# A gated MoBA-attention and mLSTM layer in split float32 on one core: another place for the stationary weights in their buffers, and another schedule for three side jobs

## The chip, the cores and the metric

One core of a Trainium2 chip. A core has TensorE (PE, matmuls, with weight loads shown as PEld), VectorE (DVE), ScalarE (ACT), GpSimd (POOL) and SyncE (SP, which here only issues transfers). Each works through its own instructions in order; they meet at semaphores. The metric is the device time of one execution in microseconds, the median over runs.

## What is computed

The layer has one batch, 256 tokens, width 1024, and all weights are float32. Cut to what matters:

```
ada = c @ w_ada + b_ada;  shift, scale, gate = split(ada)
h   = rmsnorm(x) * (1 + scale) + shift
qa ka va za qm km vm zm om ig fg ga gm = split(h @ w_in)
ya  = (attention(rmsnorm(qa), rmsnorm(ka), va) * silu(za)) @ w_att_proj
qm, km = split(silu(causal_conv4(concat(qm, km))))
hm  = rmsnorm(sigmoid(om) * mlstm(qm, km, vm, ig, fg))
ym  = (hm * silu(zm)) @ w_ml_proj
out = x + gate * ((sigmoid(ga) * ya + sigmoid(gm) * ym) @ w_out)
```

With 256 tokens, attention is causal attention over one block with a relative bias.

## The kernel before, in words

**Split products.** Every large product is made of three float32r matmuls: each operand is split into a high part and the rest (`wh`, `wl` of the weights, `hTh`, `hTl` of h), and high x high, rest x high and high x rest are summed. ScalarE makes `wh` by a cast of the loaded `raw` tile (line 501), VectorE makes `wl = raw - wh` (line 505), or GpSimd for the eight steps in `pool_lo`.

**Steps.** After a first phase (norm, modulation, the projections qa and ka) the work is a list `place` of steps. A step is 256 rows of the contraction by 512 columns of weights; `split(g + 4)` prepares step g + 4 while step g's matmuls are issued. The order of the segments is va (3 parts), za, qm, km, att, zm, vm, then om mixed with the first half of ga, then ga, gm, ml, out. A segment has two halves of 512 columns with four steps each. Steps are numbered from va's first: za starts at 12, qm at 20, km at 28, att at 36, zm at 44, vm at 52.

**Two ways round.** In za, qm, km, att, ga, gm and ml (`kind="ws"`) the weights are stationary: a step has 24 matmuls, each with a weight load of 128 x 128 from `wh` or `wl` and 256 columns of h (or of ya in att, of ym in ml) moving (lines 1160, 1162, 1163). In va, zm, vm and om the weights move, 512 columns at a time (lines 1153 to 1155, 1136 to 1138), and out goes by 256 columns (lines 1146, 1173 to 1175).

**Buffers.** `wh` and `wl` have five buffers each of `RING` = 1152 floats, of which 1024 are used; for `ws` steps the used part begins at float `WS_AT`, so at byte 320 of the buffer. In the built program every such buffer begins at a multiple of 512 bytes, `hTh` and `hTl` 256 bytes past one, and `yah`, `yal`, `ymh`, `yml` at one. So a stationary tile lies 64 bytes (modulo 512) beyond its moving one in the projections of h, and 320 beyond in att and ml. In out, the stationary `yh` and `yl` lie at 64 and 192 and the moving weights at 0. There are six `raw` tiles of 1 MB; SyncE fills them in a fixed order, a load going out when the last reader of the tile it takes over is done.

**Accumulators.** PSUM holds two accumulators `mm` for segment halves. The one of att's first half is that of km's first half, free when km's first half has been convolved. `conv` (line 718) does this in two parts q of 2 x 128 channels: ScalarE starts the sum (line 729), VectorE adds three shifted taps for two channel groups, six instructions (line 735).

**Hooks.** Side jobs hang on steps with `at(step, fn, ...)`; they are issued after `split` and ahead of the step's matmuls. Three of them are touched by the change:

- *Output gate.* `gate_init` (line 947) spreads c over the partitions. `gate_acc(j)` (line 952) is one VectorE reduction over 128 x 1024 (line 954) of the gate's weights with c; there are eight, two for each of four 1 MB loads, and a load's `raw` tile is free after its second reduction. `GSEG` says ahead of which segments the loads stand, and the reductions come four and three steps ahead of those segments.
- *Sums of h.* om is computed by seven block products instead of eight; for that `h_full` (two VectorE sums) and `h_sum` (four) form sums of blocks of h, which `h_high` and `h_low` split in vm.
- *Sums of om's weights.* `om_sum` (line 762) forms sums of weight blocks in DRAM by transfers that GpSimd issues: plain copies (line 769) and adding ones (line 767), eight sums of two halves each, `OM_SUMS`. Later ones read earlier ones; the first reader in SBUF comes with om.

Of the kernel before, what the change touches and what calls it, by code (L numbers as in the profile page):

```python
# [21 lines left out]
NEG = -1e30  # L22
BUCKETS = 32

RING, WS_AT = 1152, 80

COL = dict(qa=0, ka=1024, va=2048, za=3072, qm=4096, km=5120, vm=6144, zm=7168, om=8192,
           ig=9216, fg=9220, ga=9224, gm=10248)
# [23 lines left out]
OM_FIRST = (0, 1, 4, 5)  # L52
OM_SUMS = ((0, (0, 0), False), (2, (0, 1), False), (0, (0, 1), True), (2, (1, 1), True),
           (1, 0, False), (1, (1, 1), True), (3, 1, False), (3, (1, 0), True))
OM_SUM_AT = 6
W_PIECES = ((0, 512), (512, NR), (512, 1024), (1024, NR))


# [13 lines left out]
def tile_hybrid(ctx: ExitStack, tc: tile.TileContext, x, c, params2, w_row, w_va, ada_mod, ada_gate,  # L72
# [62 lines left out]
    adat, wrow, wsp, hf = {}, {}, {}, {}  # L135
# [102 lines left out]
    for j in range(4):  # L238
        n, q = divmod(j, 2)
        nc.tensor.matmul(pc[:, n, q * 256:(q + 1) * 256], pick[:, j:j + 1].to_broadcast([128, 128]), cparts,  # L240
                         start=q == 0, stop=q == 1, skip_group_check=True)
# [129 lines left out]
    def start(name, half=0):  # L371
        return G0[C[name, half]]

    def done(name, half):
        return GE_[C[name, half]]
# [6 lines left out]
    def add_load(fn):  # L382
        loads.append(fn)
        return len(loads) - 1

    def raw_tile():
        return rawp.tile([128, 2048], F32, name="raw")
# [3 lines left out]
    def mk_single(i, q):  # L391
        def f():
            v = raw_tile()[:, 0:4 * NV]
            nc.sync.dma_start(v, w_va[i, q])
            return v.rearrange("p (k n) -> p k n", k=4)
        return f

    def mk_pair(src, c0, kp):
        def f():
            t = raw_tile()  # L400
            v = t.rearrange("p (k n) -> p k n", k=2)
            nc.sync.dma_start(v, src[:, 2 * kp:2 * kp + 2, c0:c0 + 1024])
            return v
        return f

    def mk_quad(src, c0, q):
        def f():
            v = raw_tile().rearrange("p (k n) -> p k n", k=4)
            nc.sync.dma_start(v, src[:, 4 * q:4 * q + 4, c0:c0 + 512])
            return v  # L410
        return f
# [7 lines left out]
    def mk_block(blk):  # L419
        def f():  # L420
            v = raw_tile().rearrange("p (k n) -> p k n", k=4)
            if isinstance(blk, int):
                for hf in range(2):
                    nc.sync.dma_start(v[:, 2 * hf:2 * hf + 2], om_sums[blk][hf])
            else:
                nc.sync.dma_start(v, om_block(*blk))
            return v
        return f

    NSINGLE = 3  # L430
    GSEG = ("km", "att", "zm", "vm")
    gate_loads = []
    for g, (i, kp) in enumerate(place):
        ch = chunks[i]
        if kp == 0 and ch["name"] in GSEG and ch["half"] == 0:
            gate_loads.append(add_load(mk_pair(ada_gate, 0, len(gate_loads))))
        if ch["kind"] == "sums":
            if kp == 0:
                add_load(mk_block(ch["blk"]))
            raw_of[g] = (len(loads) - 1, slice(2 * kp, 2 * kp + 2), slice(0, 512))  # L440
        elif i < NSINGLE or ch["name"] == "ga":
            if kp % 2 == 0:
                quad[i] = add_load(mk_single(i, kp // 2) if i < NSINGLE else mk_quad(ch["src"], ch["c0"] + 512 * ch["half"], kp // 2))
            raw_of[g] = (quad[i], slice(2 * (kp % 2), 2 * (kp % 2) + 2), slice(0, ch["n"]))
        else:
            if ch["half"] == 0:
                pair[ch["name"], kp] = add_load(mk_pair(ch["src"], ch["c0"], kp))
            c0 = 512 * ch["half"]
            raw_of[g] = (pair[ch["name"], kp], slice(0, 2), slice(c0, c0 + 512))
        last_use[raw_of[g][0]] = g  # L450
# [59 lines left out]
    def at(step, fn, *a):  # L510
        hooks.setdefault(step, []).append((fn, a))
# [466 lines left out]
    def ev_out(pt, c0, n, t):  # L978
# [6 lines left out]
        if m < n:  # L985
# [4 lines left out]
              zm=ev_zm, vm=ev_vm, ga=ev_ga, gm=ev_gm)  # L990
# [28 lines left out]
    for nm in ("qm", "km"):  # L1019
        for hf in range(2):  # L1020
            s = done(nm, hf)
# [6 lines left out]
    s = start("zm")  # L1028
    for half in range(2):
        at(s + 5 * half, ml_split, half)  # L1030
        at(s + 5 * half + 3, ml_scores, 2 * half)
        at(s + 5 * half + 4, ml_scores, 2 * half + 1)
    at(start(GSEG[0]) - 10, gate_init)
    gate_left = {}
    for q, nm in enumerate(GSEG):
        s = start(nm) - 4
        at(s, gate_acc, 2 * q)
        at(s + 1, gate_acc, 2 * q + 1)
        gate_left[s + 1] = gate_loads[q]
    at(start("ga"), gate_write)  # L1040
    at(start("gm") + 1, gate_read)
    for q in range(4):
        at(start("ml") + 3 + q, gate_columns, q)
    for q, (i, src, add) in enumerate(OM_SUMS):
        for hf in range(2):
            at(OM_SUM_AT + 5 * q + 2 * hf, om_sum, i, src, add, hf)
    T["A"] = {}
    s = start("att", 1)
    for kh in range(2):
        at(s + 1 + kh, h_full, kh)  # L1050
    for q, name in enumerate(("P5", "P7", "P6", "P3")):
        at(s + 3 + q, h_sum, name)
    s = start("vm") + 1
    for q, name in reversed(list(enumerate(("P5", "P6", "P3", "P7")))):
        at(s + q, h_high, name)
# [1 line left out]
    for hp in range(2):  # L1057
        s = done("om", 6) + 2 * hp
# [29 lines left out]
    for g in range(NG):  # L1088
        ci, kp = place[g]
        ch = chunks[ci]  # L1090
# [39 lines left out]
        for kk in range(2):  # L1130
# [8 lines left out]
            elif ch["name"] == "out":  # L1139

                for i in (0, 1):
                    for t, c0 in ((0, 0), (0, 256), (1, 0), (1, 256)):
                        a = (sh_, sl_)[i][:, k, t * 128:(t + 1) * 128]
                        cs = slice(c0, c0 + 256)
                        for w in (wh, wl)[:2 - i]:
                            nc.tensor.matmul(mmt[ci][:, t, cs], a, w[:, kk, cs],  # L1146
                                             start=first and i == 0 and c0 == 0 and w is wh,
# [82 lines left out]
```

## Time and profile before

| | us |
|---|---|
| median of 3 runs | 351.18 |
| lowest, highest | 350.91, 352.48 |
| the profiled execution | 352.73 |
| its span, first to last instruction | 350.9 |

The profile is of one execution. A row of the timeline has the start in us, the duration in us, the engine, the line, the operation, what it writes and reads, and in brackets how long the engine had been idle and who ended that. A matmul's end is modelled and overlaps the next one's start, so the pace of matmuls is read from start to start.

### The profile page before, as it was taken

What the parts mean: (1) busy time and instruction counts of PE and PEld (TensorE: products, weight loads), DVE (VectorE), ACT (ScalarE), POOL (GpSimd) and SP (SyncE); (2) the same over time, 40 slices, a digit from 0 to 9 for tenths busy, and PEclk for the clock granted to TensorE, in tenths of its full rate; (3) what the DMA queues carried; (4) which work ended last, traced back from release to release, by engine and by line L of the source; (5) the groups of instructions that cost most, each with busy time, mean ns of one, the idle gap of its engine ahead of it and who ended that gap; (6) DMA issues with size and microseconds to landing.
All of it is one profiled execution on the core that took longest, in us unless ns stands there. A gap on an engine that the chain in (4) does not pass through costs nothing.

```text
span 350.9 us, 6244 instructions
## 1 busy us (share of the span) xinstructions
PE 344.8 (98%) x2420; PEld 322.6 (92%) x2420; DVE 265.2 (76%) x393; ACT 220.1 (63%) x344; POOL 99.1 (28%) x97
## 2 busy tenths in 40 slices
PE   7999999999999999999999999999999999999995
PEld 7787889999999999999998888888989999999995
DVE  6989987976993439878988895777777456789842
ACT  4868789799777866574627374668573463565410
POOL 4700003953403473674405172000002131202000
PEclk9999999999999999999999999999999999999999
DMA  8999999894794978799799856677999027444011
GB/s 300 416 414 415 414 418 419 241 391 146 256 325 140 241 200 280 232 389 272 269 337 347 294 193 227 224 277 274 144 283 375 4 75 299 168 169 192 2 62 60
DMA packets 29069, 89.33 MB, mean 255 GB/s; under 512 B 3368, under 2 KB 5296, under 8 KB 28336
## 3 DMA queue, kind: packets, MB, share of 16 engines
q1 hardware_dynamic: 26008, 80.02, 63.1%
q0 software_dynamic: 2880, 8.39, 10.3%
q10 hardware_dynamic: 152, 0.53, 0.5%
q8 instruction: 19, 0.31, 0.3%
q14 instruction: 10, 0.08, 0.1%
HBM read 87.68 MB, written 9.64 MB: 277 GB/s over the span
## 4 chain that ended last, share of the span: by engine, by line
PE 91%; DVE 4%; ACT 2%; issue 1%; POOL 1%; POOLq 0%; ACTq 0%; DVEq 0%
PE mm L1160 13%; PE pm L203 13%; PE mm L1162 13%; PE mm L1163 13%; PE mm L1153 6%; PE mm L1154 6%; PE mm L1155 6%; PE mm L1146 3%; PE aux L1136 2%; PE aux L1137 2%; PE aux L1138 2%; DVE kmT L735 1%; PE xps L268 1%; PE aux L695 1%; PE mm L1174 1%; PE mm L1175 1%
## 5 line engine op out<-in xcount | busy, mean ns | idle before, releaser
L505 DVE TENSOR_TENSOR wl<-raw,wh 128x1024 fp32r<-128x1024 f32 (+1 forms) x98 | 123.7, 1281 | 50.3 <-ACT wh L501 50.1
L501 ACT CAST wh<-raw 128x1024 fp32r<-128x1024 f32 (+1 forms) x106 | 105.5, 1015 | 30.8 <-PE mm L1155 12.0
L1160 PE MATMUL mm<-hTh,wh 128*128 128x256 f32 x320 | 90.2, 282 | 0.0
L1163 PE MATMUL mm<-hTh,wl 128*128 128x256 f32 x320 | 88.9, 278 | 0.0
L1162 PE MATMUL mm<-hTl,wh 128*128 128x256 f32 x320 | 88.9, 278 | 0.0
L1162 PEld LDWEIGHTS mm<-hTl,wh 128*128 128x128 f32 x320 | 60.3, 189 | 0.2
L1160 PEld LDWEIGHTS mm<-hTh,wh 128*128 128x128 f32 x320 | 60.3, 188 | 0.2
L1163 PEld LDWEIGHTS mm<-hTh,wl 128*128 128x128 f32 x320 | 60.1, 188 | 0.0
L1153 PE MATMUL mm<-wh,hTh 128*128 128x512 f32 (+1 forms) x112 | 40.5, 362 | 0.0
L1154 PE MATMUL mm<-wl,hTh 128*128 128x512 f32 (+1 forms) x112 | 40.2, 359 | 0.0
L1155 PE MATMUL mm<-wh,hTl 128*128 128x512 f32 (+1 forms) x112 | 40.2, 359 | 0.0
L505 POOL TENSOR_TENSOR wl<-raw,wh 128x1024 fp32r<-128x1024 f32 x8 | 21.0, 2631 | 15.8 <-ACT wh L501 15.8
L1155 PEld LDWEIGHTS mm<-wh,hTl 128*128 128x128 f32 x112 | 21.0, 188 | 2.5
L1153 PEld LDWEIGHTS mm<-wh,hTh 128*128 128x128 f32 x112 | 21.1, 188 | 2.4
L1154 PEld LDWEIGHTS mm<-wl,hTh 128*128 128x128 f32 x112 | 21.1, 188 | 2.4
L188 ACT CAST wrh<-raw 128x512 fp32r<-128x512 f32 (+1 forms) x24 | 18.2, 761 | 8.0 <-DMA raw<-in_w_row_dram 8.0
L193 DVE TENSOR_TENSOR wrl<-raw,wrh 128x512 fp32r<-128x512 f32 (+1 forms) x26 | 20.5, 813 | 1.3 <-ACT wrh L188 1.3
L203 PE MATMUL pm<-wrh,hTh 128*128 128x512 f32 x64 | 20.0, 393 | 0.0
L203 PE MATMUL pm<-wrh,hTl 128*128 128x512 f32 x64 | 19.9, 392 | 0.0
L841 POOL TENSOR_TENSOR attT<-attT,gat 128x1024 f32<-128x1024 f32 x2 | 5.3, 2635 | 50.3 <-ACT gat L840 50.3
L203 PE MATMUL pm<-wrl,hTh 128*128 128x512 f32 x64 | 19.3, 396 | 0.0
L1160 PE MATMUL mm<-yah,wh 128*128 128x256 f32 x64 | 18.1, 282 | 0.4 <-DVE kmT L735 0.4
(244 smaller groups left out, 753.3 us busy)
## 6 DMA issues: line engine op xcount, KB each, us to landing
raw<-in_w_in_dram SPq DMA_DIRECT2D x31, 1024.0 KB, 8.1
adat<-in_ada_mod_dram SPq DMA_DIRECT2D x16, 512.0 KB, 8.8
om_sum<-in_w_in_dram POOLq DMA_DIRECT2D x12, 512.0 KB, 8.8
raw<-in_w_va_dram SPq DMA_DIRECT2D x6, 688.0 KB, 8.9
raw<-in_ada_gate_dram SPq DMA_DIRECT2D x4, 1024.0 KB, 8.9
raw<-in_w_att_proj_dram SPq DMA_DIRECT2D x4, 1024.0 KB, 8.2
raw<-om_sum SPq DMA_DIRECT2D x8, 512.0 KB, 4.3
raw<-in_w_ml_proj_dram SPq DMA_DIRECT2D x4, 1024.0 KB, 5.8
```

Of the source, the lines that this page charges most:

```text
L188: copy(wsp[k][0][:, c0:c1], wrow[k][:, c0:c1])
L193: e.tensor_tensor(l[:, cs], wrow[k][:, cs], h[:, cs].bitcast(F32), op=OP.subtract)
L203: nc.tensor.matmul(pm[ch][:, t], a[:, k, t * 128:(t + 1) * 128], b[:, cs], start=k == 0 and i == 0, stop=k == KT - 1 and i == 2)
L501: nc.scalar.copy(h, w)
L505: e.tensor_tensor(l, w, h.bitcast(F32), op=OP.subtract)
L1146: nc.tensor.matmul(mmt[ci][:, t, cs], a, w[:, kk, cs], start=first and i == 0 and c0 == 0 and w is wh, stop=last and i == 1 and c0 > 0, sk ...
L1153: nc.tensor.matmul(o, a, wh[:, kk], start=first, stop=False)
L1154: nc.tensor.matmul(o, a, wl[:, kk], start=False, stop=False)
L1155: nc.tensor.matmul(o, b, wh[:, kk], start=False, stop=last)
L1160: nc.tensor.matmul(o, wh[:, kk, cs], sh_[:, k], start=first and i % 2 == 0, stop=False, skip_group_check=True)
L1162: nc.tensor.matmul(o, wh[:, kk, cs], sl_[:, k], start=False, stop=False, skip_group_check=True)
L1163: nc.tensor.matmul(o, wl[:, kk, cs], sh_[:, k], start=False, stop=last and i % 2 == 1, skip_group_check=True)
```

## The change

It does four things.

1. `WS_AT` goes from 80 to 96 floats: stationary weights begin at byte 384 of their buffers. A stationary tile then lies 128 bytes (modulo 512) beyond its moving one in the projections of h, 384 in att and ml. The buffers stay where they are, and so does every other tile.
2. The gate's four loads stand ahead of qm (two), zm and vm instead of km, att, zm and vm, and the reductions are hung on steps 20 and 21, 22 and 23, 40 and 41, 44 and 45; before, on 24 and 25, 32 and 33, 40 and 41, 48 and 49.
3. `h_full` goes from steps 41 and 42 to 25 and 29, `h_sum` from 43 to 46 to 37, 39, 41 and 43.
4. The sums in DRAM get a step each from a list: first halves at 5, 8, 11, 14, 20, 26, 32, 38, second halves three steps later; before, at 6, 11, 16 and so on to 41, second halves two steps later.

```
-RING, WS_AT = 1152, 80
+RING, WS_AT = 1152, 96
...
-OM_SUM_AT = 6
+OM_SUM_AT = (5, 8, 11, 14, 20, 26, 32, 38)
...
-    GSEG = ("km", "att", "zm", "vm")
+    GSEG = ("qm", "qm", "zm", "vm")
...
-        if kp == 0 and ch["name"] in GSEG and ch["half"] == 0:
-            gate_loads.append(add_load(mk_pair(ada_gate, 0, len(gate_loads))))
+        if kp == 0 and ch["half"] == 0:
+            for _ in range(GSEG.count(ch["name"])):
+                gate_loads.append(add_load(mk_pair(ada_gate, 0, len(gate_loads))))
...
-    at(start(GSEG[0]) - 10, gate_init)
+    at(start("qm") - 2, gate_init)
     gate_left = {}
-    for q, nm in enumerate(GSEG):
-        s = start(nm) - 4
+    for q, s in enumerate((start("qm"), start("qm") + 2, start("att", 1), start("zm"))):
         at(s, gate_acc, 2 * q)
         at(s + 1, gate_acc, 2 * q + 1)
         gate_left[s + 1] = gate_loads[q]
...
-    for q, (i, src, add) in enumerate(OM_SUMS):
+    for (i, src, add), step in zip(OM_SUMS, OM_SUM_AT):
         for hf in range(2):
-            at(OM_SUM_AT + 5 * q + 2 * hf, om_sum, i, src, add, hf)
+            at(step + 3 * hf, om_sum, i, src, add, hf)
     T["A"] = {}
-    s = start("att", 1)
     for kh in range(2):
-        at(s + 1 + kh, h_full, kh)
+        at(start("qm", 1) + 1 + 4 * kh, h_full, kh)
     for q, name in enumerate(("P5", "P7", "P6", "P3")):
-        at(s + 3 + q, h_sum, name)
+        at(start("att") + 1 + 2 * q, h_sum, name)
```

In the changed kernel the lines between the load list and the hooks (437 to 1033) have numbers one higher, and those behind the hooks (from 1053 on, the matmuls among them) one lower.

TensorE and ScalarE have the same instructions in the same order before and after. VectorE's order at the convolutions of km's first half, before (`ISA raw,gcol` is a gate reduction, followed by the read of its sum; `wl` belongs to `split`):

```order
194 L735 SCALAR_TENSOR_TENSOR kmT<-mm,prm_68,kmT 128x255 x2
195 L735 SCALAR_TENSOR_TENSOR kmT<-mm,prm_68,kmT 128x254 x2
196 L735 SCALAR_TENSOR_TENSOR kmT<-mm,prm_68,kmT 128x253 x2
197 L954 ISA raw,gcol<-raw,cbg,prm_68 128x1024
198 L954 ISA gcol 128x1
199 L505 TENSOR_TENSOR wl<-raw,wh 128x1024
200 L735 SCALAR_TENSOR_TENSOR kmT<-mm,prm_68,kmT 128x255 x2
201 L735 SCALAR_TENSOR_TENSOR kmT<-mm,prm_68,kmT 128x254 x2
202 L735 SCALAR_TENSOR_TENSOR kmT<-mm,prm_68,kmT 128x253 x2
203 L954 ISA raw,gcol<-raw,cbg,prm_68 128x1024
```

and at the same place after:

```order
200 L736 SCALAR_TENSOR_TENSOR kmT<-mm,prm_68,kmT 128x255 x2
201 L736 SCALAR_TENSOR_TENSOR kmT<-mm,prm_68,kmT 128x254 x2
202 L736 SCALAR_TENSOR_TENSOR kmT<-mm,prm_68,kmT 128x253 x2
203 L506 TENSOR_TENSOR wl<-raw,wh 128x1024
204 L736 SCALAR_TENSOR_TENSOR kmT<-mm,prm_68,kmT 128x255 x2
205 L736 SCALAR_TENSOR_TENSOR kmT<-mm,prm_68,kmT 128x254 x2
206 L736 SCALAR_TENSOR_TENSOR kmT<-mm,prm_68,kmT 128x253 x2
```

The reductions between and behind the two convolutions have left. VectorE at the start of qm's convolutions, before (`yf` is attention's product with the gate za):

```order
169 L701 TENSOR_TENSOR yf<-aux,zat 128x512
170 L505 TENSOR_TENSOR wl<-raw,wh 128x1024
171 L701 TENSOR_TENSOR yf<-aux,zat 128x512
172 L505 TENSOR_TENSOR wl<-raw,wh 128x1024
173 L701 TENSOR_TENSOR yf<-aux,zat 128x512
174 L735 SCALAR_TENSOR_TENSOR qmT<-mm,prm_68,qmT 128x255 x2
```

and after:

```order
172 L506 TENSOR_TENSOR wl<-raw,wh 128x1024
173 L702 TENSOR_TENSOR yf<-aux,zat 128x512
174 L955 ISA raw,gcol<-raw,cbg,prm_68 128x1024
175 L955 ISA gcol 128x1
176 L506 TENSOR_TENSOR wl<-raw,wh 128x1024
177 L702 TENSOR_TENSOR yf<-aux,zat 128x512
178 L955 ISA raw,gcol<-raw,cbg,prm_68 128x1024
179 L955 ISA gcol 128x1
180 L955 ISA raw,gcol<-raw,cbg,prm_68 128x1024
181 L955 ISA gcol 128x1
182 L736 SCALAR_TENSOR_TENSOR qmT<-mm,prm_68,qmT 128x255 x2
```

Four reductions now stand ahead of qm's first convolution: three in these rows, and the first two rows further up, behind the `yf` before. SyncE's loads from za's third on, before (`md` and `NM` belong to the mLSTM's gates):

```order
40 L402 DMA raw<-in_w_in_dram 128x2x1024 x6
41 L402 DMA raw<-in_ada_gate_dram 128x2048
42 L402 DMA raw<-in_w_in_dram 128x2x1024
43 L620 DMA md<-G 4x256
44 L626 DMA NM<-md 128x4x256
45 L402 DMA raw<-in_w_in_dram 128x2x1024 x3
46 L402 DMA raw<-in_ada_gate_dram 128x2048
```

and after:

```order
40 L402 DMA raw<-in_w_in_dram 128x2x1024 x2
41 L402 DMA raw<-in_ada_gate_dram 128x2048 x2
42 L402 DMA raw<-in_w_in_dram 128x2x1024 x4
43 L621 DMA md<-G 4x256
44 L627 DMA NM<-md 128x4x256
45 L402 DMA raw<-in_w_in_dram 128x2x1024 x4
46 L402 DMA raw<-in_w_att_proj_dram 128x2x1024 x4
```

Two gate loads moved ahead of the four of qm, and none stands between km and att. In the built program the third km load takes the tile that the second reduction leaves, and att's first load that of the fourth.

## The prediction

> **What bounds the kernel now.** I read the page first: how long TensorE is busy, and at which clock.
>
> ```profile
> span 350.9 us, 6244 instructions
> PE 344.8 (98%) x2420; PEld 322.6 (92%) x2420; DVE 265.2 (76%) x393; ACT 220.1 (63%) x344; POOL 99.1 (28%) x97
> PEclk9999999999999999999999999999999999999999
> ```
>
> TensorE is busy for 98% of the span at the full clock, so the other engines matter only where they make it wait, and what is left is how fast matmuls follow one another. The list of TensorE's waits has three lines, two of them at the very start:
>
> ```profile
> PE warm L232 <- POOL ident masks.py:199: 1.4, 1, 1.4
> PE xps L268 <- ACT diag L251: 0.6, 1, 0.6
> PE mm L1160 <- DVE kmT L735: 0.4, 1, 0.4
> ```
>
> The third is the only one in the main part, where km ends and att begins. Next I asked for the matmuls in order of time, in a stretch of qm (first two rows), in att (next two), and at the end of an earlier qm step (last two). All are the same instruction: 256 columns, its own weight load before it.
>
> ```profile
> 129.81 0.28 PE L1160 MATMUL mm<-hTh,wh 128*128 128x256 f32 x1
> ...
> 133.89 0.28 PE L1160 MATMUL mm<-hTh,wh 128*128 128x256 f32 x1
> ```
> ```profile
> 165.76 0.28 PE L1162 MATMUL mm<-yal,wh 128*128 128x256 f32 x1
> ...
> 168.94 0.28 PE L1162 MATMUL mm<-yal,wh 128*128 128x256 f32 x1
> ```
> ```profile
> 116.82 0.28 PE L1163 MATMUL mm<-hTh,wl 128*128 128x256 f32 x1
> ...
> 117.18 0.28 PE L1163 MATMUL mm<-hTh,wl 128*128 128x256 f32 x1
> ```
>
> In the first stretch 36 matmuls lie between the rows, 4.08 us, or 113.3 ns each. In att 27 take 3.18 us, 117.8 ns each. In the last, three take 0.36 us, 120 ns by rows rounded to 10 ns. So there are two paces, 4.5 ns apart, and the qm projection shows both. The durations carry the same mark, 276 ns at the fast pace and 281 at the slow one. By line, with least, median and most:
>
> ```profile
> L1162 PE MATMUL mm<-hTl,wh x320: 275/276/287, 83.5 to 302.5; 128*128 128x256 f32 x160
> L1162 PE MATMUL mm<-yal,wh x64: 281/281/282, 161.5 to 183.8; 128*128 128x256 f32 x64
> L1162 PE MATMUL mm<-yml,wh x64: 281/281/282, 302.8 to 325.1; 128*128 128x256 f32 x64
> ```
> ```profile
> L1173 PE MATMUL mm<-wh,yh x32: 276/276/277, 336.3 to 346.8; 128*128 128x256 f32 x32
> ```
>
> att and ml run at the slow pace from first to last; the end of out, whose stationary operand lies elsewhere, runs at the fast one; the projections from h are mixed. For their mixture I take the mean of the whole group:
>
> ```profile
> L1163 PE MATMUL mm<-hTh,wl 128*128 128x256 f32 x320 | 88.9, 278 | 0.0
> L1162 PE MATMUL mm<-hTl,wh 128*128 128x256 f32 x320 | 88.9, 278 | 0.0
> ```
>
> 278 lies two fifths of the way from 276 to 281, so some 0.4 of the 960 matmuls with h as moving operand are slow. A fixed set of operands goes at both paces, so the pace is not set by addresses alone: it holds for long stretches, and something at a stretch's start chooses it.
>
> **The change, part by part.** The sum is made against the profiled execution: 352.73 us, of which 350.9 are the span and 1.8 lie around it. The median of the three runs is 351.18, 1.55 below; I take each difference off the median.
>
> *Gate reductions and the stall.* VectorE in order of time at the end of km, GpSimd beside it, and TensorE:
>
> ```profile
> 152.56 2.43 DVE L735 SCALAR_TENSOR_TENSOR kmT<-mm,prm,kmT 128x255 f32<-128x255 f32 x6 [2.43 <-ACT kmT L729]
> 154.91 2.78 DVE L954 CUSTOM_DVE_ANT_0 raw<-raw,cbg,prm 128x1024 f32<-128x1024 f32 x1
> 157.62 1.21 DVE L505 TENSOR_TENSOR wl<-raw,wh 128x1024 fp32r<-128x1024 f32 x1
> 158.76 2.42 DVE L735 SCALAR_TENSOR_TENSOR kmT<-mm,prm,kmT 128x255 f32<-128x255 f32 x6
> 161.10 1.27 DVE L954 CUSTOM_DVE_ANT_0 raw<-raw,cbg,prm 128x1024 f32<-128x1024 f32 x1
> ```
> ```profile
> 153.72 2.88 POOL L505 TENSOR_TENSOR wl<-raw,wh 128x1024 fp32r<-128x1024 f32 x1
> 156.07 1.55 POOL L767 DMA_DIRECT2D om_sum<-in_w_in_dram  x1
> ```
> ```profile
> 160.64 0.28 PE L1163 MATMUL mm<-hTh,wl 128*128 128x256 f32 x1
> 161.32 0.36 PE L1160 MATMUL mm<-yah,wh 128*128 128x256 f32 x1 [0.41 <-DVE kmT L735]
> 161.52 0.28 PE L1162 MATMUL mm<-yal,wh 128*128 128x256 f32 x1
> ```
>
> att's first accumulator is the one that km's first half leaves, and the second convolution of that half ends at 158.76 + 2.42 = 161.18, since a reduction of 2.78 us stood in front of it, drawn out beside GpSimd's work: the next one, with nothing beside it, took 1.27. TensorE's gap is 0.68 us where 0.11 is normal, and the next is 0.20 where att's pace is 0.12: 0.57 + 0.08 = 0.65 us lost. The change takes both reductions out of this place. The convolution then ends up to 2.78 us earlier, at 158.4. VectorE's wl, now beside GpSimd in its turn, may be drawn out by the same 1.5 us, which leaves 159.9, still before the last km matmul at 160.64. The stall goes: -0.65.
>
> *Where the reductions go.* Four now stand behind qm's start:
>
> ```profile
> 118.51 1.23 DVE L505 TENSOR_TENSOR wl<-raw,wh 128x1024 fp32r<-128x1024 f32 x1 [2.64 <-ACT wh L501]
> ...
> 124.16 1.49 DVE L505 TENSOR_TENSOR wl<-raw,wh 128x1024 fp32r<-128x1024 f32 x1 [3.82 <-ACT wh L501]
> 125.57 0.68 DVE L701 TENSOR_TENSOR yf<-aux,zat 128x512 f32<-128x512 f32 x1
> ```
> ```profile
> 132.59 2.54 DVE L954 CUSTOM_DVE_ANT_0 raw<-raw,cbg,prm 128x1024 f32<-128x1024 f32 x1
> 136.20 2.42 DVE L735 SCALAR_TENSOR_TENSOR qmT<-mm,prm,qmT 128x255 f32<-128x255 f32 x6
> ```
> ```profile
> 138.99 0.28 PE L1160 MATMUL mm<-hTh,wh 128*128 128x256 f32 x1
> ```
>
> The first falls into VectorE's 2.64 us of idle before 118.51, the second into the 3.82 before 124.16: nothing. The third and fourth begin at 126.25 and take 2 x 1.27 = 2.5 us, or 2 x 2.78 = 5.6 us if GpSimd's work draws both out, so they end between 128.8 and 131.8. Queued behind them are qm's convolutions, which free the accumulator for km's first matmul, at about 139.0; until now they ended at 136.20 + 2.42 = 138.62. Late by 1.6 us at worst, they get back the reduction that stood between them, 2.54 us here and at least 1.27, so they end at most 0.3 us later than before, inside the slack of 138.99 - 138.62 = 0.4 us. I take zero; the bounds are 0, since TensorE waits for nothing there now, and +0.3, if that slack is gone.
>
> The two h_full sums (1.2 us, the price of any 128x1024 pass on VectorE by the row at 157.62) take the place of reductions at qm's second convolution and stand alone behind the fourth, where 2.4 us of idle follow (the bracket at 152.56). h_sum moves out of zm. Zero each.
>
> *Loads.* The two gate loads now stand ahead of qm's on SyncE's queue, so qm's last weights leave when km's first did, and all adds of the sums in DRAM but the last ones come earlier.
>
> ```profile
> 97.69 0.37 SPq L402 DMA_DIRECT2D raw<-in_w_in_dram  x1
> ```
> ```profile
> DMA to landing us min/median/max: 3.4/7.9/13.1
> ```
> ```profile
> 111.36 1.05 ACT L501 CAST wh<-raw 128x1024 fp32r<-128x1024 f32 x1 [0.23 <-ACT yah L702]
> ```
> ```profile
> q0 software_dynamic: 2880, 8.39, 10.3%
> ```
>
> 97.69 + 7.9 = 105.6, at most 110.8; ScalarE casts this piece at 111.36, and TensorE needs it four steps later. The sums cost the transfers 0.103 x 350.9 / 16 = 2.3 us of all engines each, and two more now fall into this stretch; even 4.5 us late, four steps of 24 x 113 ns = 2.7 us cover it. The later km loads wait for the first reductions (third km load) and for the fourth (first att load), and all loads behind them wait too; TensorE needs them in steps 30 and 36, no earlier than 139.0 + 2 x 2.7 = 144, over 10 us after those reductions end. Zero, bounds 0 and +0.5.
>
> *The offset.* 64 bytes more changes no instruction. All it can change is which pace the 1344 matmuls with streamed stationary weights run at. No row of before shows this offset, so I bound it from both sides by 4.5 ns: if all become fast, 0.4 x 960 x 4.5 ns = 1.7 us in the projections and 384 x 4.5 = 1.7 in att and ml are saved, -3.4; if all become slow, 0.6 x 960 x 4.5 = 2.6 us are lost. I take zero for the offset itself: with operands 64 bytes apart both paces occur, so 64 more need not decide it.
>
> But the stall bears on the pace. Up to 160.64 TensorE ran fast without a break; after it, att ran slow for all 192 matmuls. Without a stall nothing interrupts the fast run, and I expect it to carry on into att: 192 x 4.5 ns = 0.86 us. The nearest rows for and against: the end of out shows that the fast pace holds over many steps (276/276/277), att's that the slow one does.
>
> The Trainium skill, "TensorE: Matmul & The Clock Gate", section "Step-by-step: what each phase is for", says that TensorE reads the streamed operand and the weights through two independent ports, so that loading weights takes nothing from a running matmul. By that rule no offset could matter. The trace does not settle it: it shows two paces for one form of instruction, which the rule does not name, but not that addresses choose between them.
>
> Sum: -0.65 - 0.86 = -1.5 us, 351.18 - 1.5 = 349.7.
>
> **Rivals.**
> *All matmuls fast.* The new offset lets every stretch settle at 113.3 ns, as the end of out does with its own offset: -0.65 - 3.4, 347.1 us. For it: out's stationary tiles lie at places chosen apart from the others and stay fast. Against: half of what it needs is in att and ml, whose offset to their moving operand differs from that of the projections, before and after.
> *All slow.* With 384 bytes no stretch leaves the slow pace, as none in att and ml does now: -0.65 + 2.6, about 353.1 us, slower. It decides as soon as more than 0.65 / 0.0045 = 144 of the now fast matmuls turn slow. For it: att and ml show 384 matmuls in a row that never settled. Against: the projections do settle, in most stretches.
> *Only the stall.* The pace in att has nothing to do with the stall and the offset does nothing: -0.65, 350.5 us. The rule of the Trainium skill on two ports (same page and section) would give this time too.
>
> **How the numbers follow.** The forecast gets 0.38, with its own range 348.9 to 350.6; all fast 0.30 (one lucky offset would pay in both groups); all slow 0.18; only the stall 0.14. The range leaves out the far third of all fast and of all slow, under 2 in 10: 346.9 to 353.2. About 0.5%, 1.75 us, is what a measurement of this kernel can tell from no change. Below 349.4 lie 0.28 from all fast, 0.16 from the forecast and 0.01 from the last: 0.45. Above 352.9 lie two thirds of all slow: 0.12. The rest, 0.43, is within.
>
> **What would show it.** In the profile after: no line of TensorE waiting for kmT; no reduction between km's convolutions; yal's and yml's rows with 276 or 281 ns; the mean of the h groups, 276 if all fast, 281 if all slow, 278 if mixed as now. A wait of TensorE on qmT at about 139 would show the reductions in the wrong place, one on a raw tile the loads. I am wrong if the stall is gone and the time is above 351.2, or if att is still at 281 without a stall before it.

## The result: slower by 1.5%

The changed kernel takes 356.49 us (median of five runs, 356.24 to 357.13), the kernel before 351.18 (350.91 to 352.48): a ratio of 1.0149, interval 1.0127 to 1.0171. The forecast was 349.7, with 353.2 as its upper end.

Three lines from the head of the page of the kernel after, and its complete list of TensorE's waits (us in total, times, longest):

```profile
span 354.6 us, 6241 instructions
PE 348.4 (98%) x2420; PEld 327.1 (92%) x2420; DVE 262.8 (74%) x393; ACT 221.8 (63%) x344; POOL 100.9 (28%) x97
PEclk9999999999999999999999999999999999999999
```
```profile
PE warm L232 <- POOL ident masks.py:199: 1.4, 1, 1.4
PE aux L641 <- ACT GE L619: 1.1, 1, 1.1
PE xps L268 <- ACT diag L251: 0.2, 1, 0.2
```

The wait for kmT is gone, as forecast; a new one stands in its place, in which TensorE waits 1.1 us for the exponential of the gates (`GE`). TensorE is busy for 3.6 us longer with the same 2420 matmuls at the same clock. The groups of the `ws` steps, whose weights are stationary, show where (busy us, mean ns of one): the three that have h as moving operand (the h groups) and one of att:

```profile
L1159 PE MATMUL mm<-hTh,wh 128*128 128x256 f32 x320 | 91.4, 286 | 0.0
L1162 PE MATMUL mm<-hTh,wl 128*128 128x256 f32 x320 | 90.2, 282 | 0.0
L1161 PE MATMUL mm<-hTl,wh 128*128 128x256 f32 x320 | 90.1, 282 | 0.0
L1161 PE MATMUL mm<-yal,wh 128*128 128x256 f32 x64 | 18.0, 281 | 0.0
```

The h groups had a mean of 278 (L1163 and L1162 of the kernel before). A duration counts the overlap with the neighbours, so the time from one start to the next, the spacing, is the better measure: in the stretch of qm that ran at 113.3 ns before, nine matmuls lie between these two rows of the kernel after, ten spacings in 1.19 us or 119 ns each:

```profile
130.74 0.28 PE L1159 MATMUL mm<-hTh,wh 128*128 128x256 f32 x1
...
131.93 0.28 PE L1161 MATMUL mm<-hTl,wh 128*128 128x256 f32 x1
```

Both kernels issue the same matmuls in the same order, so the starts of the two traces can be subtracted one by one. Taken over all neighbouring pairs of the 1344 `ws` matmuls with nothing between them (spacings under 160 ns, so that waits stay out), what lies above 113.3 ns adds up to 3.15 us before and 7.18 us after: +4.03 us of pace. Beside it stand +1.17 us at L641 (1.37 us from start to start instead of 0.20), -0.64 at the stall on kmT (0.56 and 0.08), and three smaller differences, -0.33 in the first 36 us, -0.26 at 193 us and -0.28 at 293 us. The sum is +3.69, and the spans differ by 354.6 - 350.9 = 3.7. The medians differ by 5.3, since the profiled execution of before was 1.55 us above its median, while that of after is at its median.

### The profile page after: what moved, and what is told of

Same layout as the page of the kernel before. It is cut to its first block, busy times and chain, and to the rows that moved or that the text cites. A ratio compares the mean times of both kernels' runs of the same rounds, so it can differ in the third digit from the quotient of the medians.

```text
span 354.6 us, 6241 instructions
## 1 busy us (share of the span) xinstructions
PE 348.4 (98%) x2420; PEld 327.1 (92%) x2420; DVE 262.8 (74%) x393; ACT 221.8 (63%) x344; POOL 100.9 (28%) x97
## 4 chain that ended last, share of the span: by engine, by line
PE 87%; DMA 4%; ACT 4%; DVE 3%; issue 0%; SPq 0%; ACTq 0%
PE mm L1162 13%; PE mm L1161 13%; PE mm L1159 13%; PE pm L203 12%; PE mm L1152 5%; PE mm L1153 5%; PE mm L1154 5%; PE mm L1145 3%; DMA raw<-in_w_in_dram 3%; PE aux L1135 2%; PE aux L1136 2%; PE aux L1137 2%; DVE wl L506 1%; DMA xt<-in_x_dram 1%; ACT wh L502 1%; PE xps L268 1%
## 5 line engine op out<-in xcount | busy, mean ns | idle before, releaser
L506 DVE TENSOR_TENSOR wl<-raw,wh 128x1024 fp32r<-128x1024 f32 (+1 forms) x98 | 121.2, 1253 | 55.1 <-ACT wh L502 54.4
L1159 PE MATMUL mm<-hTh,wh 128*128 128x256 f32 x320 | 91.4, 286 | 0.0
L1162 PE MATMUL mm<-hTh,wl 128*128 128x256 f32 x320 | 90.2, 282 | 0.0
L1161 PE MATMUL mm<-hTl,wh 128*128 128x256 f32 x320 | 90.1, 282 | 0.0
L1162 PEld LDWEIGHTS mm<-hTh,wl 128*128 128x128 f32 x320 | 60.3, 188 | 0.0
L1162 PE MATMUL mm<-yah,wl 128*128 128x256 f32 x64 | 18.0, 281 | 0.0
```

The lines of the kernel that those rows point to most:

```text
L506: e.tensor_tensor(l, w, h.bitcast(F32), op=OP.subtract)
L1159: nc.tensor.matmul(o, wh[:, kk, cs], sh_[:, k], start=first and i % 2 == 0, stop=False, skip_group_check=True)
L1161: nc.tensor.matmul(o, wh[:, kk, cs], sl_[:, k], start=False, stop=False, skip_group_check=True)
L1162: nc.tensor.matmul(o, wl[:, kk, cs], sh_[:, k], start=False, stop=last and i % 2 == 1, skip_group_check=True)
```

## Experiments

Two theories at first. A: the offset sets the pace. B: the offset does nothing, and the interruption at L641 leaves a slow pace behind it, as the prediction held that the stall on kmT did.

### Which part of the change

**e1**, the kernel before with the offset alone:

```
-RING, WS_AT = 1152, 80
+RING, WS_AT = 1152, 96
```

> The kernel before with the stationary weights at 384 bytes instead of 320, nothing else. Theory A (the offset sets the pace of the matmuls): the h projections run at 281 ns or more from first to last, as in the kernel after, and the time is 351.2 + 4.0 (the pace share of the difference between the two profiles) = 355 us, up to 356. Theory B (the offset does nothing; the changed schedule makes TensorE wait for L619's exponential at 106 us and that interruption leaves the slow pace behind it): 351.2 us, rows of the h groups at 278 as before. In both the stall on kmT at the end of km is there.

Measured: 355.75 us, ratio 1.0101 (1.0077 to 1.0126). No line for L641, and the h groups as in the kernel after (286, 282 and 282 ns), the first of them:

```profile
L1160 PE MATMUL mm<-hTh,wh 128*128 128x256 f32 x320 | 91.4, 286 | 0.0
```

A holds. One part of the expectation failed: the stall on kmT is gone here too, though a reduction stands where it stood. The second convolution of km's first half ends at 161.47 us, 0.3 later than before, but km's last matmul now starts at 162.83 instead of 160.64, so the convolution comes in time.

**e2**, the kernel after with the offset alone undone (`WS_AT` 80).

> The kernel after with the offset back at 320 bytes: gate, norm and DRAM sums moved as in the change. Theory A: the wait for the exponential stays (+1.2), the stall on kmT stays away (-0.65), the h groups are back at 278: about 351.7 us. Theory B: 356.5 us as the kernel after, h groups at 282.

Measured: 352.07 us, ratio 0.9989 (0.997 to 1.0007). The h groups are back at 278, the wait is there, and att is fast, which neither theory had priced:

```profile
PE aux L641 <- ACT GE L619: 1.0, 1, 1.0
```
```profile
L1161 PE MATMUL mm<-hTl,wh 128*128 128x256 f32 x320 | 88.9, 278 | 0.0
L1161 PE MATMUL mm<-yml,wh 128*128 128x256 f32 x64 | 18.0, 281 | 0.0
L1161 PE MATMUL mm<-yal,wh 128*128 128x256 f32 x64 | 17.7, 276 | 0.0
```

The ratios of e1 and e2 multiply to 1.009, less than the 1.0149 of the whole change. The kernel before had a median of 351.18 us beside the kernel after and of 352.20 beside e1 to e4, and the kernel after was not timed beside them. How much of the gap lies in the two sets of runs, and how much in the parts acting together, stays open.

**e3**, the kernel after with the sums in DRAM at their old steps (`OM_SUM_AT` 6, 11, ... 41, second halves 2 steps later).

> The kernel after (384 bytes) with the sums in DRAM at the steps of the kernel before. Both theories: the wait for the exponential at 106 us goes, because fewer adds of the sums run beside the qm loads. Theory A: only that, 356.5 - 1.2 = 355.3 us, h groups still 282. Theory B: the slow pace goes with the wait, 356.5 - 1.2 - 2.1 (the pace share between 110 and 163 us) or more: 353 us or less, h groups at 278.

Measured: 355.79 us, ratio 1.0101 (1.0077 to 1.0125), as A has it. The wait at L641 was 0.09 us in the profiled execution.

**e4**, e3 with `WS_AT` 80.

> 320 bytes and the sums in DRAM at the steps of the kernel before; only the gate reductions, their loads and the norm's sums are moved. Theory A and theory B: the stall on kmT is gone and no new wait is there: 351.2 - 0.65 = 350.5 us, faster than both kernels. If moving the two gate loads ahead of qm's is itself what delays the qm load, the wait for the exponential is still there and the time is 351.5 or more.

Measured: 352.06 us, ratio 0.9998 (0.9978 to 1.0018); the profiled execution took 354.02, so its rows show one of the longer ones. The wait is there with 1.5 us, although the sums are where they were: the sums don't make it, and the 0.09 of e3 shows how much it varies. This trace also shows a fast stretch end. VectorE's second convolution of qm's first half, drawn-out split before it, and TensorE at km's first matmul (140.34):

```profile
133.94 3.87 DVE L506 TENSOR_TENSOR wl<-raw,wh 128x1024 fp32r<-128x1024 f32 x1
137.73 2.42 DVE L736 SCALAR_TENSOR_TENSOR qmT<-mm,prm,qmT 128x255 f32<-128x255 f32 x6
```
```profile
139.32 0.28 PE L1159 MATMUL mm<-hTh,wh 128*128 128x256 f32 x1
...
140.23 0.28 PE L1162 MATMUL mm<-hTh,wl 128*128 128x256 f32 x1
140.34 0.31 PE L1159 MATMUL mm<-hTh,wh 128*128 128x256 f32 x1
140.49 0.28 PE L1161 MATMUL mm<-hTl,wh 128*128 128x256 f32 x1
140.61 0.28 PE L1162 MATMUL mm<-hTh,wl 128*128 128x256 f32 x1
```

Until 140.34 the matmuls are 113.3 ns apart; one gap of 0.15 us follows, and from there through the rest of km and all of att they are 117.8 apart. The convolution ends at 137.73 + 2.42 = 140.15, in e2 at 139.79, and there the fast pace goes on. That the gap is a late accumulator is inferred from these times; no wait is listed for it. The convolution ends 0.19 us ahead of km's first matmul here; in b1 and b2 (below) it ends 0.20 us ahead, and the same gap of 0.15 us follows; in the kernel before (0.37) and in e2 (0.65) there is none. But in b1 and b2 km is back at 113.3 ns after the gap, so such a gap can end the fast pace and need not.

### What the offset does

Theory P: the place of the stationary operand sets the pace. Theory D: its distance from the streamed operand does, that is from the moving one (h, or the `y` tiles in att and ml). The kernel after with `WS_AT` 16, 64, 112 and 128:

> The kernel after with the stationary weights 64 bytes into their buffers (out's stationary yh lies 64 bytes past a multiple of 512 and runs at 276 ns). Theory P (the place of the stationary operand within 512 bytes sets the pace): h groups, att and ml all at 276 ns and 113.3 ns apart; against the schedule at 320 bytes (352.1 us) that saves 2.5 us: 349.6 us. Theory D (the distance from the streamed operand sets it; h lies at 256, y at 0, out's streamed weights at 0): att and ml, 64 bytes from their streamed operand as out, go at 276, the h groups, 192 bytes before theirs, are not known from any row: between 349.6 us (fast) and 354.5 us (as slow as at 384).

> The kernel after with the stationary weights 256 bytes into their buffers: distance 0 from h, 256 from y. Theory P: one pace for the h groups and att and ml together, whichever it is. Theory D: the h groups (distance 0) and att and ml (distance 256) differ. From all fast to all at 384's pace: 349.6 to 356.5 us; the nearest measured offset is 320 (352.1 us), which I take.

> The kernel after with the stationary weights 448 bytes into their buffers: distance 192 from h (out's yl lies 192 bytes from its streamed operand and is fast), 448 from y. Theory D: the h groups at 276 ns, 113.3 apart, so about 350.0 to 351.0 us with att and ml unknown. Theory P: further from 320 than 384 is, slow everywhere: 356.5 us or more.

> The kernel after with the stationary weights 512 bytes into their buffers, that is at a multiple of 512 as without an offset: distance 256 from h, 0 from y. Theory P and theory D both leave it open, since no row has it; the words of the code, an offset for stationary weights alone, speak for a slow pace: 356.5 us or more. If P holds, h groups and att and ml have one pace here; if D holds, the h groups match att at 256 bytes (distance 256 both).

All streamed operands begin at a multiple of 256 bytes, so P and D differ only where one of them is moved. That was done in **m1**, `WS_AT` 128 with

```
+    consts.tile([128, 32], F32, name="pad0")
     hTh = consts.tile([128, KT, S], F32R, name="hTh")
     hTl = consts.tile([128, KT, S], F32R, name="hTl")
+    consts.tile([128, 96], F32, name="pad1")
```

> The kernel after with the stationary weights at 512 bytes (a multiple of 256, the slowest place so far: 120.0 ns between matmuls in every group), and h, the streamed operand of the projections, moved by 128 bytes, from 256 to 384 within 512; y is not moved and is the control. Theory P (place of the stationary operand alone): the h groups stay at 119.9 ns, time 357.5 us. Theory D (distance between streamed and stationary operand, period 256 bytes): the h groups go to the 118.7 ns of the kernel after, where the distance is also 128 bytes, att and ml stay at 120.0; 960 x 1.2 ns = 1.2 us less, 356.3 us. (h is also the stationary operand of the token-wise stages, whose pace it may change; that is read from their own rows.)

The four distances between were then taken on the fastest schedule found (e5, below), with `WS_AT` 72, 88, 104 and 120:

> The kernel before with the steps of the sums in DRAM of the kernel after (350.1 us at 320 bytes, the fastest so far), stationary weights at 288 bytes: distance 32 modulo 256 from every streamed operand of the projections. Distance 0 gives 120.0 ns in all stretches, distance 64 gives 113.3 or 117.8. If the pace hangs on the distance in steps of 64 bytes, 288 does as 256: 120.0 ns everywhere, 1344 x some 6 ns = 7 to 8 us more, 357.5 us. If it changes evenly with the distance: between, about 353 to 354 us. If 32 has only the fast state: 1.3 us less than 350.1, 348.8 us.

> The same at 352 bytes, distance 96. Steps of 64 bytes: as 320, 350.1 us, with the same stretches fast and slow. Evenly: between 320 (350.1) and 384 (about 355.5 with this schedule), 352 to 353 us. Only fast: 348.8 us.

> The same at 416 bytes, distance 160. Steps of 64 bytes: as 384, 118.7 ns and the cycle of six matmuls everywhere, 355.5 us. Evenly: between 384 and 448 (353.5 with the schedule of the kernel after, less the wait for the exponential and the stall, 352.5), 354 us.

> The same at 480 bytes, distance 224. Steps of 64 bytes: as 448, 117.8 ns with stretches at 113.3, 352.5 us. Evenly: between 448 and 512 (357.5 in the schedule of the kernel after), 354 to 355 us.

Mean spacing in ns (start to start, as above, in one profiled execution each), by the distance of the stationary tile from the streamed one, modulo 256. The s kernels have the schedule of the kernel after, as e2 has, and the f kernels that of e5, so times are to be compared within a schedule:

| Distance | Kernel | qm and km | att | ml | Median us | Ratio to before |
|---|---|---|---|---|---|---|
| 0 | s256 | 120.0 | 120.0 | 120.0 | 357.90 | 1.0181 (1.0165 to 1.0196) |
| 0 | s512 | 120.0 | 120.0 | 120.0 | 357.51 | 1.0178 (1.0154 to 1.0202) |
| 32 | f288 | 118.3 | 118.3 | 118.3 | 354.64 | 1.0078 (1.0065 to 1.0091) |
| 64 | s64 | 113.6 | 113.3 | 113.3 | 351.14 | 0.9996 (0.998 to 1.0013) |
| 64 | e2 | 113.6 | 113.3 | 117.8 | 352.07 | 0.9989 (0.997 to 1.0007) |
| 64 | e5 | 113.6 | 113.3 | 113.3 | 350.06 | 0.9954 (0.9937 to 0.9971) |
| 96 | f352 | 117.4 | 117.3 | 117.3 | 353.94 | 1.0059 (1.0041 to 1.0076) |
| 128 | after | 118.6 | 118.7 | 118.7 | 356.49 | 1.0149 (1.0127 to 1.0171) |
| 160 | f416 | 120.0 | 120.0 | 120.0 | 357.54 | 1.0154 (1.0135 to 1.0173) |
| 192 | s448 | 117.8 | 117.8 | 113.3 | 353.51 | 1.0056 (1.0039 to 1.0073) |
| 224 | f480 | 116.7 | 116.7 | 116.7 | 352.68 | 1.0031 (1.0018 to 1.0045) |

256 and 512 bytes give one pace, 64 and 320 the same two, and 128 another than 0: the pace repeats after 256 bytes. Only at 64 and 192 were stretches at 113.3 seen, beside others at 117.8. At 128 no stretch settles: the spacings go round in five, near 115, 118, 122, 120 and 119 ns (the expectation for 416 bytes speaks of six). s64 came to 351.14, not 349.6: its profile has att and ml fast, but also 1.3 us of the wait for the exponential, and the h groups keep the mixture of 320; that profile is of one of its shortest executions, 350.71 us. s448 fits neither theory as it was priced: h goes at 117.8 there, ml at 113.3, so a distance with a fast pace does not grant it. s256 and s512 are the slowest of all, with one pace in all groups. The expectations on steps of 64 bytes and on an even change both failed: 32 is neither like 0 nor like 64, and 160 is slower than both its neighbours, 128 and 192.

m1 decides for D. Its weight loads (PEld) and matmuls of one line, least, median and most: h, moved by 128 bytes, against att, one of the two controls that were not moved:

```profile
L1163 PEld LDWEIGHTS mm<-hTl,wh x320: 187/188/193, 85.2 to 309.0; 128*128 128x128 f32 x160
L1163 PE MATMUL mm<-hTl,wh x320: 274/281/287, 85.3 to 309.2; 128*128 128x256 f32 x160
L1163 PEld LDWEIGHTS mm<-yal,wh x64: 188/192/192, 165.9 to 188.6; 128*128 128x128 f32 x64
L1163 PE MATMUL mm<-yal,wh x64: 281/283/283, 166.0 to 188.7; 128*128 128x256 f32 x64
```

With the stationary tiles at one place for all, the matmuls on h are 118.7 ns apart (qm and km), as in the kernel after (118.6), and att and ml stay at 120.0 and 119.9. Only this one distance was made by moving h; the others of the table were made by moving the weights. The time, 359.41 us (ratio 1.0218, 1.0192 to 1.0243), missed the expected 356.3: against s512, 1.8 us were lost before 55 us, ahead of the first `ws` matmul, and some 0.65 between 218 and 247 us, in vm and om, where the weights move and h, or a sum of its blocks, is the stationary operand. What of this the shift of h makes was not separated.

In m1 the weight loads of att take 192 ns, those of h 188. Loads of 192 ns are no mark of distance 0 alone. In the kernel before, at distance 64, one of the three lines of att has them:

```profile
L1162 PEld LDWEIGHTS mm<-yal,wh 128*128 128x128 f32 x64 | 12.3, 192 | 0.0
L1163 PEld LDWEIGHTS mm<-yah,wl 128*128 128x128 f32 x64 | 12.0, 188 | 0.0
L1160 PEld LDWEIGHTS mm<-yah,wh 128*128 128x128 f32 x64 | 12.0, 188 | 0.6 <-issue 0.6
```

In the eight traces at distance 64, every att or ml at 117.8 ns has just one such line, and every one at 113.3 or 113.4 has none. At distance 192 (s448) att is at 117.8 without one.

### The stall and the wait for the exponential

**b1** and **b2**: the kernel before at 320 and at 64 bytes with

```
-        s = start(nm) - 4
+        s = start(nm) - (6 if q < 2 else 4)
```

> The kernel before (320 bytes, loads and sums as there) with the first two pairs of gate reductions two steps earlier, so that none stands between the convolutions of qm or km. The stall on kmT goes (-0.65) and att takes on km's fast pace (192 x 4.5 ns = -0.86): 351.2 - 1.5 = 349.7 us, without a wait for the exponential, since no load is moved. If the pace of att does not hang on the stall: 350.5 us.

> The same at 64 bytes. Theory P and D both put 64 and 320 bytes in one class (equal modulo 256), so 349.7 us and the same two paces; if ml is fast too, as in the one profile at 64 bytes, 192 x 4.5 ns less: 348.8 us.

Measured: 351.16 us, ratio 0.9988 (0.9974 to 1.0002), and 351.24, 0.9984 (0.9967 to 1.0). The expected gain did not come, and the stall stayed in both. In b1 att runs at 117.8 ns behind it and ml at 113.3; in b2, behind a stall of the same size, att runs at 113.4 and ml at 117.8. So a stall does not settle the pace behind it. TensorE's wait (the same in b2), and VectorE before km's convolutions, in b1:

```profile
PE mm L1160 <- DVE kmT L735: 0.2, 1, 0.2
```
```profile
149.56 1.28 DVE L954 CUSTOM_DVE_ANT_0 raw<-raw,cbg,prm 128x1024 f32<-128x1024 f32 x1
...
150.77 3.42 DVE L954 CUSTOM_DVE_ANT_0 raw<-raw,cbg,prm 128x1024 f32<-128x1024 f32 x1
...
154.12 2.42 DVE L735 SCALAR_TENSOR_TENSOR kmT<-mm,prm,kmT 128x255 f32<-128x255 f32 x6
```

The second reduction, now ahead of both convolutions, is drawn out to 3.42 us beside GpSimd's split, and the first convolution starts at 154.12 instead of 152.56.

**e5**, the kernel before with the steps of the sums in DRAM alone taken from the kernel after:

> The kernel before with nothing but the steps of the sums in DRAM taken from the kernel after. If the bunched adds at 81 to 94 us delay the qm loads, TensorE waits some 1 us for the exponential at about 105 us and the time is 352.2 us; if the two gate loads ahead of qm's are the cause, there is no such wait and the time stays at 351.2 us.

Measured: 350.06 us, ratio 0.9954 (0.9937 to 0.9971), faster than both kernels, and lower than either expectation. No wait at L641, so the bunched adds don't make it; and no stall, though the reductions stand where they stood. In e5, GpSimd and then VectorE at km's end:

```profile
150.46 4.77 POOL L505 TENSOR_TENSOR wl<-raw,wh 128x1024 fp32r<-128x1024 f32 x2 [4.21 <-ACT wh L501]
155.16 0.53 POOL L769 DMA_DIRECT2D om_sum<-om_sum  x1
```
```profile
154.62 1.69 DVE L954 CUSTOM_DVE_ANT_0 raw<-raw,cbg,prm 128x1024 f32<-128x1024 f32 x1
...
157.38 2.42 DVE L735 SCALAR_TENSOR_TENSOR kmT<-mm,prm,kmT 128x255 f32<-128x255 f32 x6
```

In the kernel before, an issue of a sum stands between GpSimd's two splits:

```profile
150.76 2.40 POOL L505 TENSOR_TENSOR wl<-raw,wh 128x1024 fp32r<-128x1024 f32 x1 [4.69 <-ACT wh L501]
153.12 1.05 POOL L767 DMA_DIRECT2D om_sum<-in_w_in_dram  x1
```

The second split starts at 153.72 there and ends at 153.72 + 2.88 = 156.60; in e5 the two follow one another and end at 150.46 + 4.77 = 155.23. The reduction ends at 154.91 + 2.78 = 157.69 before and at 154.62 + 1.69 = 156.31 in e5, 1.1 us behind the split both times, a little less than the 1.27 that it takes alone. The Trainium skill, "SBUF — State Buffer", section "Who interferes with whom", says that a VectorE instruction with two SBUF inputs contends with a GpSimd instruction that reads SBUF, that the port pair they share is an exclusive lock, and that the order of issue decides who blocks. These times agree: 1.27 us back from the reduction's end lies within 0.2 us of the split's end, as if the reduction, issued later, had waited for it.

**g1**, e2 with one edit:

```
-    GSEG = ("qm", "qm", "zm", "vm")
+    GSEG = ("km", "km", "zm", "vm")
```

> The schedule of the kernel after at 320 bytes (352.1 us, wait for the exponential 1.0 us in its profile) with one edit: both early gate loads stand behind qm's four loads on SyncE's queue instead of ahead of them; reductions and sums as there. If the order of the loads makes the wait, it goes: 352.1 - 1.0 = 351.1 us or less, ScalarE's cast at about 101 us starts without waiting for a load. If the bunched adds of the sums or the place of the reductions make it, the wait stays at about 1 us and the time at 352.1 us.

Measured: 349.62 us, ratio 0.9952 (0.9931 to 0.9973), with no wait at L641 and att and ml at 276. The order of the loads makes the wait. All nine traces with the two gate loads ahead of qm's show it, from 0.09 us (e3) to 1.5 (e4), and none of the other ten does. The chain of waits of the kernel after, in order of time (start, us, what), shows how:

```profile
92.47 10.74 DMA raw<-in_w_in_dram
...
103.29 1.06 ACT wh L502
...
104.37 1.23 DVE wl L506
105.60 0.19 DVE G L617
105.78 0.33 DVE G L618
...
106.21 0.42 ACT GE L619
...
106.68 0.31 PE aux L641 x2
```

and ScalarE's cast, in the kernel after and in g1:

```profile
103.29 1.05 ACT L502 CAST wh<-raw 128x1024 fp32r<-128x1024 f32 x1 [2.12 <-DMA raw<-in_w_in_dram]
```
```profile
101.51 1.03 ACT L502 CAST wh<-raw 128x1024 fp32r<-128x1024 f32 x1
```

The gate loads leave at 69.56 and 72.31, where g1 has two pieces of qm (70.01 and 72.75), so these pieces leave only at 87.13 and 92.47. The second lands 10.74 us later; the cast starts 1.8 us later than in g1. TensorE needs that piece only four steps on, but the gates' own work on VectorE and the exponential on ScalarE are queued behind the cast and its split, and TensorE needs the exponential at once. g1 and e5 are the versions that beat both kernels beyond the noise; between the two, 349.62 and 350.06, their intervals overlap.

## Why the prediction was wrong

**The offset, taken as zero.** This is the step that failed: "All it can change is which pace the 1344 matmuls with streamed stationary weights run at", and so "with operands 64 bytes apart both paces occur, so 64 more need not decide it". The offset cost +4.03 us in the profiles, and 1.0% by itself (e1, whose spacings add up to the same 7.18). 320 lies at one of the two distances, of the eight tried, at which a fast pace was seen, and 384 does not. The bounds failed with it: the two paces seen at one offset were taken as the ends of what any offset could give. 384 has a pace of its own, 118.7, so the loss in att and ml, which the bound put at nothing, was 0.34 us, and the projections lost more than 0.6 x 960 x 4.5 ns. The rival "all slow" came nearest in its mechanism and was too cheap at 353.1: pace 4.03 instead of 2.6, and no price for the new wait.

**The pace carried into att, -0.86.** At 320 bytes it fits four traces: in e2, e5 and g1 nothing interrupts TensorE between the end of qm and att, and att runs at 276 ns; in e4 km and att are slow from a gap of 0.15 us at km's start on. But the link to the stall is looser than the prediction had it: in b2 att runs at 113.4 ns behind a stall, and in b1 and b2 km goes on fast behind the same gap. An interruption opens the choice; what decides it is not known. At 384 there is no fast pace to carry.

**The stall, -0.65.** Its size came as forecast (0.64). The cause given was only half of it: b1 takes the reductions out from between the convolutions and the stall stays with 0.2 us, e5 leaves them there and it goes. In these traces it is the time for which GpSimd's split holds VectorE up that decides, and between before and e5 only the steps of the sums differ. The stall was a matter of 0.6 us on a path with several such terms.

**The loads, zero with +0.5 at most.** The second step that failed, +1.17. It followed qm's last piece, with 7.9 us of flight, to TensorE's use of it. The piece that hurt was an earlier one that flew 10.74 us, and what suffered was not its matmuls but the work queued behind its cast.

**The reductions at qm, zero.** In the kernel after the second convolution of qm's first half ends in time. e4 shows how near this was: 0.36 us later than in e2, a gap of 0.15 us followed, and the fast pace was gone. The bound of +0.3 left out that a gap can cost more than its own length.

**The base.** The terms were read from an execution of 352.73 us and taken off the median, 351.18. That the execution at the median had the stall and the slow att, no run shows. The miss of 6.8 us is the pace (4.0), the 0.9 in att that did not come, the wait (1.2), and the 1.6 by which the medians lie further apart than the profiles, less the three smaller differences (0.9).

**The rule on two ports.** The Trainium skill, "TensorE: Matmul & The Clock Gate", section "Step-by-step: what each phase is for", has weight loads and moving operands read through independent ports, without loss to a running matmul. The prediction drew from it that no offset could matter, and that is not what these runs show: with everything else equal, the distance between the two operands changes the spacing from 113.3 to 120.0 ns (att and ml in s64 and s256). Whether it is the ports that make it, no run shows.

## What to carry to other kernels

An offset that costs no instruction is not free: where TensorE is 98% busy with matmuls that each load new weights, time a few distances between the stationary and the streamed operand before anything else, and don't bound an untried one by the paces of a tried one. When loads are reordered, follow every piece that is delayed, not the last, and ask what is queued behind the instruction that waits for it. A prediction of some 1 us over a path with several waits of that size needs the neighbour that draws an instruction out (here GpSimd) in its sum.

## What the runs showed of the hardware

The spacing of these float32r matmuls with 256 columns, a new weight load before each, hangs on the distance between their two operands, modulo 256 bytes: 120.0 ns at 0 and at 160, 116.7 to 118.7 at 32, 96, 128 and 224. At 64 and 192 two states were seen, 113.3 and 117.8. The longest unbroken stretch at 113.3 has 523 spacings (g1, qm to att). A gap of 0.15 us ended the fast pace in e4, and a gap of the same length did not in b1 and b2. At distance 0 the weight loads of att and ml take 192 ns instead of 188 on all three lines (s256, s512, m1), and at distance 64 on one line of three wherever att or ml is at 117.8. What chooses between the two states after an interruption, and what in the memory or the array makes the distance matter, stays open.
